# Latent attention: the score scale moved into the query norm's root, row maxima formed negated, and the stage's first twelve products spread over both PSUM bank sets

## The chip, the cores and the metric

The kernel runs on one core of a Trainium2 chip. A core has TensorE (matrix products, written into PSUM), VectorE, ScalarE and GpSimd (element by element work), and DMA queues that bring weights from memory. PSUM has eight banks of 128 x 512 float32 values here. The metric is the device time of one execution in microseconds (us); the median of several runs is compared.

## The reference

The program is a two-layer streaming encoder step: 512 new frames with 16 meta tokens in front (the prompt), and 32 frames of a running stream with 256 past frames (the sample). Each layer is a half-step feed-forward block, a mixer and another half-step feed-forward block. The mixer of the first layer is a gated linear attention; that of the second is a multi-head latent attention (MLA), which the change concerns:

```python
cq, ckv, kr = split(xn @ w_down, ...)            # 384, 256, 64 columns
q = (rmsnorm(cq, q_norm) @ w_uq).reshape(B, L, 8, 128 + 64)
q_nope, q_rope = q[..., :128], apply_rope(q[..., 128:], pos)
ckv = rmsnorm(ckv, kv_norm); kr = apply_rope(kr, pos)
q_lat = einsum('blhn,rhn->blhr', q_nope, w_uk)
s = (q_lat . keys_lat + q_rope . keys_rope) * scale      # scale = 192 ** -0.5
p = softmax(where(mask, s, -inf))
o = einsum('bhqk,bkr->bqhr', p, keys_lat)                # then w_uv and w_out
```

The mask is causal in chunks of 64 frames. The score is linear in the query, and the query is linear in the root 1/sqrt(mean square) of its norm, one number for each frame.

## The kernel before

All activations stand feature by frame: 128 partitions by 560 columns (512 prompt frames, 32 sample frames, 16 meta tokens). Every float32 product is made of three matmuls on operands split into a high and a low part (lines 429, 430 and 432 in `mm`, 436 to 438 in `mm3`); `split` (lines 381, 382) makes the two parts, a ScalarE cast and a VectorE subtraction. Columns are worked in two halves (272 each for queries, `HALF_Q`; 264 each for keys).

PSUM in the mixers is two sets of tiles in one pool: `ps` with three banks, for large products, and `s` with five, for scores, transposes and small things. `self.bank()` asks for one of `ps`, `self.bank("s")` for one of `s`. A tile of a set waits until an earlier tile of the same set has been read.

The MLA goes: latent, rotary key and query projections; `query_roots` and `query_norm` for each half (sum of squares by TensorE, `rsqrt` on VectorE, transposes on TensorE to spread the root over all partitions, a ScalarE copy into `yq` at line 1174, and two GpSimd products at line 1176 that fold the root into the cosine and sine tables). The norm's root is not multiplied into the projections' input but into each query product when it is read from PSUM: `plain` (line 1246) with `yq`, `rotary` through the cosine and sine tables (`rope`, lines 1043 to 1048).

`attention` then runs over eight heads. Its opening is a fixed list: keys of head 0 (two products), the second half's `query_roots`, keys of head 1 (two), `query_norm`, two pieces of the values of heads 0 and 1, and `queries(0)` (for each half a rotary product of both heads and a plain product of each): twelve products through `self.bank()`. Then come the scores of head 0 for its four query tiles, with the other three values pieces and `queries(1)` between. After that, each head's list alternates its transposes with the next head's scores, and `weave` spreads the remaining work (keys, values, queries of later heads, the sample's steps, output projection) between them.

`softmax` takes a tile of scores in PSUM (two tiles for the last query tile, which has 528 keys): the row maximum on VectorE (line 1057), the maximum of two parts (1059), times minus the scale (1060), the exponential on ScalarE with that as bias and the scale as factor, summing as it goes (1062), the sums' addition (1065), reciprocal (1066), and the product with it (1068). It is called 34 times: 32 tiles of the prompt and two of the sample.

The program's lines give priorities; the framework orders the instructions of each engine when the program is built, by what it estimates to be ready. So an engine's order in the trace is not always that of the lines: matmuls of two products can be mixed.

Of the kernel before, what the change touches and what calls it, by code (L numbers as in the profile page):

```python
# [13 lines left out]
AF = mybir.ActivationFunctionType  # L14
ALU = mybir.AluOpType
AX = mybir.AxisListType
# [19 lines left out]
SCALE = (128 + 64) ** -0.5  # L36
# [302 lines left out]
class Net:  # L339
# [18 lines left out]
    def psum(self, ffn):  # L358
# [3 lines left out]
        else:  # L362
# [3 lines left out]
                                                             reuse_waits="tile"))  # L366
        self.bufs = dict(Y=2) if ffn else dict(ps=3, s=5)

    def bank(self, tag="ps"):
        if tag not in self.bufs:  # L370
            tag = "Y"
        return self.ps.tile([P, 512], F32, name=tag, tag=tag, bufs=self.bufs[tag])
# [287 lines left out]
    def down(self, i, l, gi, acts, halves, order, after=None):  # L660
# [4 lines left out]
        def piece(m, hf):  # L665
# [3 lines left out]
            n, c = c1 - c0, slice(c0, c1)  # L669
            Y = self.bank()  # L670
            self.mm(Y[:, :n], L[m], 0, acts, halves[hf])
            nc.vector.scalar_tensor_tensor(self.h[:, m, c], Y[:, :n], 0.5, self.h[:, m, c], op0=ALU.mult, op1=ALU.add)  # L672
            if after is not None:
# [72 lines left out]
    def gla(self, xs, begin, side, op, xpool):  # L746
# [6 lines left out]
        if True:  # L753
# [17 lines left out]
            def wout(g):  # L771
# [10 lines left out]
                for m, hf in order:  # L782
                    if m // 2 not in L:
                        L[m // 2] = self.load(("go", g, m // 2))
                    c0, c1 = HALF_T[hf]
                    Y = self.bank()
                    self.mm(Y[:, :c1 - c0], L[m // 2], 4 * (m % 2), outs[2 * g] + outs[2 * g + 1], (c0, c1))
# [264 lines left out]
    def softmax(self, pool, p, parts):  # L1052

        nc = self.nc
        st = pool.tile([P, 8], F32, name="st", tag="st", bufs=4)
        for i, (s, n, c) in enumerate(parts):
            nc.vector.reduce_max(st[:, i:i + 1], s[:, :n], axis=AX.X)
        if len(parts) == 2:
            nc.vector.tensor_tensor(st[:, 0:1], st[:, 0:1], st[:, 1:2], op=ALU.max)
        nc.vector.tensor_scalar(st[:, 2:3], st[:, 0:1], -SCALE, None, op0=ALU.mult)  # L1060
        for i, (s, n, c) in enumerate(parts):
            nc.scalar.activation(p[:, c:c + n], s[:, :n], AF.Exp, bias=st[:, 2:3], scale=SCALE,
                                 accum_out=st[:, 3 + i:4 + i])
        if len(parts) == 2:
            nc.vector.tensor_tensor(st[:, 3:4], st[:, 3:4], st[:, 4:5], op=ALU.add)
        nc.vector.reciprocal(st[:, 5:6], st[:, 3:4])
        n = sum(q[1] for q in parts)
        nc.vector.tensor_scalar(p[:, :n], p[:, :n], st[:, 5:6], None, op0=ALU.mult)
# [35 lines left out]
    def mla(self, xs, turn, side):  # L1104

        nc, tc, a = self.nc, self.tc, self.a
# [5 lines left out]
        if True:  # L1112
            two = gone("ml2", 2)
            kp = brief("mlk")
            if True:
# [9 lines left out]
                norms = {}  # L1125
# [12 lines left out]
                for hf, (c0, c1) in enumerate(HALF_T):  # L1138
                    n = c1 - c0
                    for m in range(2):  # L1140
                        Y = self.bank(("s", "ps")[hf])
# [7 lines left out]
                for hf, (c0, c1) in enumerate(HALF_T):  # L1149
                    n = c1 - c0  # L1150
                    Y = self.bank()
# [15 lines left out]
                yq = self.np_.tile([P, T], F32, name="yn", tag="yn")  # L1167
# [3 lines left out]

                def query_norm(hf):
                    c = slice(*HALF_Q[hf])
                    nc.scalar.copy(yq[:, c], norms.pop(hf)())
                    for t in (self.cos, self.sin):
                        nc.gpsimd.tensor_tensor(t[:, c], t[:, c], yq[:, c], op=ALU.mult)

                L = [self.load(("wd", 3 + m)) for m in range(2)]
                for hf, (c0, c1) in enumerate(HALF_Q):
                    n = c1 - c0  # L1180
                    for m in range(3):
                        if m == 2 and len(L) == 2:
                            L.append(self.load(("wd", 5)))
                        Y = self.bank()
                        self.mm(Y[:, :n], L[m], 0, xs, (c0, c1))
                        if hf == 1 and m < 2:
                            (query_roots, query_norm)[m](0)
                        nc.vector.tensor_tensor(cq[:, m, c0:c1], Y[:, :n], xs.y[:, c0:c1], op=ALU.mult)
                        w = nv[:, wq + m:wq + m + 1]
                        nc.scalar.activation(cqh[:, m, c0:c1], cq[:, m, c0:c1], AF.Copy, scale=w)  # L1190
                        nc.vector.scalar_tensor_tensor(cql[:, m, c0:c1], cq[:, m, c0:c1], w,
                                                       cqh[:, m, c0:c1].bitcast(F32), op0=ALU.mult, op1=ALU.subtract)
                        self.square(cq[:, m, c0:c1], n, hf, m == 0)
# [4 lines left out]
            brief.close()  # L1198
            cqs = [(cqh[:, m, :], cql[:, m, :]) for m in range(3)]
            self.attention(gone, two, cqs, yq, [partial(f, 1) for f in (query_roots, query_norm)], kph, kpl, rph, rpl, ksh, ksl, rsh, rsl, kth, ktl, turn)  # L1200

    def attention(self, gone, two, cqs, yq, query_norm, kph, kpl, rph, rpl, ksh, ksl, rsh, rsl, kth, ktl, turn):
        nc, tc, a = self.nc, self.tc, self.a
# [11 lines left out]
        for t in ee:  # L1215
            nc.gpsimd.memset(t[64:, :].bitcast(F32), 0.0)
        q = {}

        def queries(pr):
            ha, hb = 2 * pr, 2 * pr + 1  # L1220
            W = {}

            def rotary(c0, c1):
                if "r" not in W:
                    W["r"] = self.load(("qr", pr))
                    W["n"] = self.load(("qn", pr))
                    for h in (ha, hb):
                        q[h] = (self.xtile(), self.xtile(), self.xtile())
                n = c1 - c0
                c = slice(c0, c1)  # L1230
                Y = self.bank()
                self.mm(Y[:, :n], W["r"], 0, cqs, (c0, c1))
                qa, qb = self.temp("y"), self.temp("sq")
                self.rope(qb, self.temp("acc"), qa[:64, :n], Y, n, (c0, c1), True)
                for x, h in ((qa, ha), (qb, hb)):
                    r = q[h][2]
                    nc.scalar.copy(r[:64, c], x[:64, :n])
                    nc.vector.tensor_tensor(r[64:, c], x[:64, :n], r[:64, c].bitcast(F32), op=ALU.subtract)

            def plain(j, h, c0, c1):  # L1240
                n = c1 - c0
                c = slice(c0, c1)
                Y = self.bank()
                self.mm(Y[:, :n], W["n"], 3 * j, cqs, (c0, c1))
                qf = self.temp(("vh", "t")[j])
                nc.vector.tensor_tensor(qf[:, :n], Y[:, :n], yq[:, c], op=ALU.mult)
                self.split(q[h][0][:, c], q[h][1][:, c], qf[:, :n])

            return [f for c in HALF_Q for f in (partial(rotary, *c), partial(plain, 0, ha, *c), partial(plain, 1, hb, *c))]

        oS = {}
# [91 lines left out]
        def keys(h):  # L1343
            def half(c0, c1):
                if c0 == 0:
                    kt[h] = two.tile([P, KP], F32R, name="kh", tag="kh"), two.tile([P, KP], F32R, name="kl", tag="kl")
                    W.append(self.load(("uk", h)))
                kh, kl = kt[h]
                Y = self.bank()
                self.mm(Y[:, :c1 - c0], W[0], 0, [(kph[:, r, :], kpl[:, r, :]) for r in range(2)], (c0, c1))  # L1350
                self.split(kh[:, c0:c1], kl[:, c0:c1], Y[:, :c1 - c0])

            W = []
            return [partial(half, 0, KP // 2), partial(half, KP // 2, KP)]

        def values(pr):
            def piece(i):
                if i == 0:
                    W.append(self.load(("uvp", pr)))
                vh, vl = ve  # L1360
                n = P if i < 4 else 64
                c = slice(i * P, i * P + n)
                Y = self.bank()
                for r in range(2):
                    w = tuple(t[:, 2 * r:2 * r + 2, :].rearrange("p a b -> p (a b)") for t in W[0])
                    self.mm3(Y[:n, :256], (kph[:, r, c], kpl[:, r, c]), w, r == 0, r == 1)
                self.split(vh[:n, i, :], vl[:n, i, :], Y[:n, :256])

            W = []
            return [partial(piece, i) for i in range(5)]  # L1370
# [395 lines left out]
```

## Time and profile before

| what | value |
|---|---|
| median of 3 runs | 2033.72 us (2029.69, 2033.72, 2036.91) |
| profiled execution, its own time | 2032.48 us |
| its span, first to last instruction | 2030.7 us |
| mean granted TensorE clock | 0.996 |
| busy: TensorE, VectorE, ScalarE, GpSimd | 2005.6, 1600.0, 1021.6, 53.5 us |
| DMA, mean over the span | 87 GB/s from and to memory |
| L1057, row maxima | 42 operations, median 0.408 us |
| L1060, times minus the scale | 34 operations, median 0.144 us |
| L1174, copy of the root | 2 operations, median 0.384 us |

Rows of the profile name line, engine and operation, the tile written, the tiles read, shape and count; times are in us, in the groups by line also in ns. "[1.80 <-DVE vl L382]" means that the engine stood idle for 1.80 us before this instruction, and that the VectorE instruction of line 382 that writes `vl` came last. PE is TensorE, PEld its weight loads, DVE VectorE, ACT ScalarE, POOL GpSimd, SP the queue that issues DMAs. A matmul's duration in a row is its latency; in a row of matmuls the next starts before the former ends. PEclk is the clock that TensorE was granted, as a share of full speed.

### The profile page before, as it was taken

The page shows a single profiled execution, that of the slowest core. Times are in us where ns is not written, and L with a number is a line of the kernel's source. Part 1 is how long each engine was busy: PE and PEld are TensorE (multiplying, and loading weights), DVE is VectorE, ACT ScalarE, POOL GpSimd, SP SyncE. Part 2 cuts the span into 40 slices and gives each one's busy share as a digit, 9 for nine tenths or more (in the row PEclk, how much of TensorE's full clock was granted, in tenths as well). Part 3 has the DMA queues.
Part 4 walks back from the last instruction along what each step waited for, and adds up shares of the span by engine and source line. Part 5 has one row for each costly group of instructions (what it writes and reads, how often), then busy time and mean ns, then how long its engine had stood idle before and what let it go on. Part 6 is the DMA issues. An engine that isn't in the chain of part 4 may idle for free.

```text
span 2030.7 us, 38170 instructions
## 1 busy us (share of the span) xinstructions
PE 2005.6 (99%) x15422; PEld 1976.2 (97%) x15422; DVE 1600.0 (79%) x2995; ACT 1021.6 (50%) x1862; POOL 53.5 (3%) x121
## 2 busy tenths in 40 slices
PE   9999999999999999999999999999999999999998
PEld 9999999989999999999999999999989999999998
DVE  8878788566558988788788877886798898888884
ACT  7444445465446544444555444454576575444453
POOL 0000000111110000000000000000110000000000
PEclk9999999999999999999999999999999999999999
DMA  5232322222222132323313333323111413333221
GB/s 184 77 109 85 104 84 81 80 81 71 68 86 92 66 107 90 98 84 105 104 51 106 100 94 95 98 75 98 60 56 44 146 31 100 110 94 98 95 74 66
DMA packets 91969, 180.16 MB, mean 89 GB/s; under 512 B 10176, under 2 KB 22080, under 8 KB 91792
## 3 DMA queue, kind: packets, MB, share of 16 engines
q1 hardware_dynamic: 87328, 172.48, 26.6%
q10 hardware_dynamic: 4464, 5.24, 0.8%
q8 instruction: 121, 1.98, 0.4%
q14 instruction: 56, 0.46, 0.1%
HBM read 173.69 MB, written 3.99 MB: 87 GB/s over the span
## 4 chain that ended last, share of the span: by engine, by line
PE 81%; DVE 12%; DMA 2%; ACT 2%; issue 1%; POOL 0%; SPq 0%; DVEq 0%; ACTq 0%; POOLq 0%
PE Y L432 8%; PE Y L429 8%; PE Y L430 8%; PE A L430 5%; PE A L432 5%; PE A L429 5%; PE ps L429 4%; PE C L432 4%; PE C L430 4%; PE C L429 4%; PE ps L432 4%; PE ps L430 4%; PE B L430 3%; PE B L432 3%; PE B L429 3%; DVE wlo L382 3%
## 5 line engine op out<-in xcount | busy, mean ns | idle before, releaser
L429 PE MATMUL Y<-ah,whi 128*128 128x280 f32 (+1 forms) x1408 | 373.7, 292 | 2.7 <-ACT ah L381 2.2
L430 PE MATMUL Y<-ah,wlo 128*128 128x280 f32 (+1 forms) x1408 | 372.8, 291 | 0.0
L382 DVE TENSOR_TENSOR wlo<-fr,whi 128x1024 fp32r<-128x1024 f32 (+1 forms) x298 | 357.9, 1211 | 15.9 <-ACT whi L381 15.6
L381 ACT CAST whi<-fr 128x1024 fp32r<-128x1024 f32 (+1 forms) x298 | 308.8, 1045 | 103.7 <-PE C L432 40.3
L430 PE MATMUL A<-x,wlo 128*128 128x280 f32 (+1 forms) x1024 | 271.7, 291 | 1.9 <-DVE wlo L382 1.8
L429 PE MATMUL A<-x,whi 128*128 128x280 f32 (+1 forms) x1024 | 272.2, 291 | 1.0 <-ACT x L181 1.0
L429 PEld LDWEIGHTS Y<-ah,whi 128*128 128x128 f32 x1408 | 265.4, 189 | 3.8 <-ACT ah L381 3.2
L672 DVE SCALAR_TENSOR_TENSOR h<-Y,h 128x280 f32<-128x280 f32 (+1 forms) x320 | 141.1, 444 | 159.0 <-PE Y L432 158.5
L430 PEld LDWEIGHTS Y<-ah,wlo 128*128 128x128 f32 x1408 | 266.3, 189 | 0.0
L382 DVE TENSOR_TENSOR wlo<-raw,whi 128x512 fp32r<-128x512 f32 (+5 forms) x231 | 195.0, 846 | 74.8 <-ACT whi L381 69.9
L381 ACT CAST whi<-raw 128x512 fp32r<-128x512 f32 (+5 forms) x231 | 169.6, 736 | 160.1 <-PE ps L432 47.5
L432 PE MATMUL Y<-al,whi 128*128 128x280 f32 (+1 forms) x1408 | 233.0, 291 | 0.0
L300 DVE TENSOR_TENSOR fr<-fr 128x1024 f32<-128x1024 f32 x160 | 195.2, 1220 | 19.5 <-DMA fr<-W 18.1
L432 PEld LDWEIGHTS Y<-al,whi 128*128 128x128 f32 x1408 | 199.4, 188 | 0.0
L430 PEld LDWEIGHTS A<-x,wlo 128*128 128x128 f32 x1024 | 192.7, 188 | 2.8 <-DVE wlo L382 2.8
L429 PEld LDWEIGHTS A<-x,whi 128*128 128x128 f32 x1024 | 192.6, 188 | 1.9 <-ACT x L181 1.2
L430 PE MATMUL B<-x,wlo 128*128 128x280 f32 (+1 forms) x704 | 186.5, 291 | 0.6 <-DVE wlo L382 0.4
L429 PE MATMUL B<-x,whi 128*128 128x280 f32 (+1 forms) x704 | 186.8, 291 | 0.1
L430 PE MATMUL C<-x,wlo 128*128 128x280 f32 (+1 forms) x704 | 186.0, 290 | 0.0
L429 PE MATMUL C<-x,whi 128*128 128x280 f32 (+1 forms) x704 | 186.0, 290 | 0.0
L432 PE MATMUL A<-x,whi 128*128 128x280 f32 (+1 forms) x1024 | 172.9, 290 | 0.6 <-DVE x L182 0.6
L536 ACT COPY r<-A 128x560 f32<-128x560 f32 (+1 forms) x120 | 74.8, 623 | 159.0 <-PE A L432 158.1
(419 smaller groups left out, 4151.7 us busy)
## 6 DMA issues: line engine op xcount, KB each, us to landing
fr<-W SPq DMA_DIRECT2D x351, 256.0 KB, 3.4
raw<-W SPq DMA_DIRECT2D x80, 512.0 KB, 3.5
raw<-W SPq DMA_DIRECT2D x100, 256.0 KB, 2.9
raw<-W SPq DMA_DIRECT2D x40, 128.0 KB, 2.1
raw<-W SPq DMA_DIRECT2D x4, 384.0 KB, 3.0
h<-xT SPq DMA_DIRECT2D x2, 560.0 KB, 6.5
o_y<-h SPq DMA_DIRECT2D x4, 272.0 KB, 2.3
o_y<-h ACTq DMA_DIRECT2D x4, 272.0 KB, 2.5
```

The costliest lines, as they stand in the source:

```text
L300: self.net.nc.vector.tensor_tensor(r[out], r[x], r[y], op=ALU.add)
L381: self.nc.scalar.copy(hi, src)
L382: self.nc.vector.tensor_tensor(lo, src, hi.bitcast(F32), op=ALU.subtract)
L429: f(hi[:, b0 + k, :], xh[:, c], start=not more and k == 0, stop=False)
L430: f(lo[:, b0 + k, :], xh[:, c], start=False, stop=False)
L432: f(hi[:, b0 + k, :], xl[:, c], start=False, stop=k == n - 1)
L536: nc.scalar.copy(r[:, :, :n], of[:, :, :n])
L672: nc.vector.scalar_tensor_tensor(self.h[:, m, c], Y[:, :n], 0.5, self.h[:, m, c], op0=ALU.mult, op1=ALU.add)
```

## The change

The score scale is multiplied into the query norm's root (`query_norm`), and reaches the scores through `yq` and the scaled cosine and sine tables. `softmax` then needs no scale: the row maxima are formed negated, the two parts are joined by a minimum, and the result is the exponential's bias at once. In `attention` a local `bank()` gives the first twelve products that ask for one the sets ps, s, s, ps, s, s, and so on (four times `ps`, eight times `s`), and `ps` to all later ones; the query, key and value products use it.

```diff
@@ softmax
         for i, (s, n, c) in enumerate(parts):
-            nc.vector.reduce_max(st[:, i:i + 1], s[:, :n], axis=AX.X)
+            nc.vector.reduce_max(st[:, i:i + 1], s[:, :n], axis=AX.X, negate=True)
         if len(parts) == 2:
-            nc.vector.tensor_tensor(st[:, 0:1], st[:, 0:1], st[:, 1:2], op=ALU.max)
-        nc.vector.tensor_scalar(st[:, 2:3], st[:, 0:1], -SCALE, None, op0=ALU.mult)
+            nc.vector.tensor_tensor(st[:, 0:1], st[:, 0:1], st[:, 1:2], op=ALU.min)
         for i, (s, n, c) in enumerate(parts):
-            nc.scalar.activation(p[:, c:c + n], s[:, :n], AF.Exp, bias=st[:, 2:3], scale=SCALE,
-                                 accum_out=st[:, 3 + i:4 + i])
+            nc.scalar.activation(p[:, c:c + n], s[:, :n], AF.Exp, bias=st[:, 0:1], accum_out=st[:, 3 + i:4 + i])
@@ query_norm
-                    nc.scalar.copy(yq[:, c], norms.pop(hf)())
+                    nc.scalar.activation(yq[:, c], norms.pop(hf)(), AF.Copy, scale=SCALE)
@@ attention
+        tags = [("ps", "s", "s")[i % 3] for i in range(12)]
+
+        def bank():
+            return self.bank(tags.pop(0) if tags else "ps")
@@ rotary and plain (in queries), half (in keys), piece (in values)
-                Y = self.bank()
+                Y = bank()
```

More of the change, by code (lines that the diff above doesn't have):

```diff
@@ L1242, in plain @@
                 c = slice(c0, c1)
-                Y = self.bank()
+                Y = bank()
                 self.mm(Y[:, :n], W["n"], 3 * j, cqs, (c0, c1))
@@ L1348, in half @@
                 kh, kl = kt[h]
-                Y = self.bank()
+                Y = bank()
                 self.mm(Y[:, :c1 - c0], W[0], 0, [(kph[:, r, :], kpl[:, r, :]) for r in range(2)], (c0, c1))
@@ L1362, in piece @@
                 c = slice(i * P, i * P + n)
-                Y = self.bank()
+                Y = bank()
                 for r in range(2):
```

## The prediction

> **What bounds the kernel now.** I read the page first: engine totals and the chain that ended last.
>
> ```profile
> span 2030.7 us, 38170 instructions
> PE 2005.6 (99%) x15422; PEld 1976.2 (97%) x15422; DVE 1600.0 (79%) x2995; ACT 1021.6 (50%) x1862; POOL 53.5 (3%) x121
> PE 81%; DVE 12%; DMA 2%; ACT 2%; issue 1%; POOL 0%; SPq 0%; DVEq 0%; ACTq 0%; POOLq 0%
> ```
>
> TensorE is the bound over the whole span: only 25.1 us (2030.7 - 2005.6) are without a matmul. A change that leaves the matmuls alone can win only where TensorE stands still or runs slowly. So next I cut the attention stage, which holds every edited line, into stretches; then one cut around the clock's dip.
>
> ```profile
> core 0: us, PE busy (x) PEld busy (x) DVE busy (x) ACT busy (x) POOL busy (x), PEclk, DMA share, GB/s
> 1456.00:1476.00 20.00, 18.07 (x140) 17.02 (x139) 16.68 (x46) 13.98 (x34) 7.69 (x19) 1.00 0.21 58
> 1476.00:1486.00 10.00, 10.00 (x66) 9.98 (x67) 8.65 (x30) 6.75 (x20) 0.78 (x1) 0.83 0.38 113
> 1486.00:1520.00 34.00, 31.20 (x221) 28.37 (x219) 32.21 (x106) 26.34 (x76) 4.76 (x13) 1.00 0.11 32
> 1520.00:1560.00 40.00, 39.82 (x308) 38.90 (x309) 34.22 (x110) 24.60 (x74) 1.45 (x5) 1.00 0.24 72
> 1560.00:1600.00 40.00, 38.01 (x287) 36.48 (x286) 37.88 (x111) 26.76 (x72) 3.10 (x9) 1.00 0.26 78
> sum 164.00, PE 157.10 PEld 149.91 DVE 145.20 ACT 108.05 POOL 17.78; mean PE 26.18 PEld 24.99 DVE 24.20 ACT 18.01 POOL 2.96
> ...
> 1477.00:1480.50 3.50, 3.50 (x16) 3.48 (x15) 2.72 (x11) 2.44 (x8) 0.09 (x1) 0.51 0.52 154
> ```
>
> Over 1456 to 1620 TensorE is without a matmul for 6.9 us (164.0 - 157.1; counted by weight loads 14.1). From 1477.0 to 1480.5 it ran at a granted clock of 0.51, which costs 3.5 x 0.49 = 1.7 us. So 6.9 + 1.7 = 8.6 us, 0.4% of the time, is what this stage can give; by weight loads 15.8. In 1486 to 1520 and 1560 to 1600 VectorE is 95% busy (32.21 of 34, 37.88 of 40): there it sets the pace. Then the waits, to see who is late.
>
> ```profile
> PE ps L429 <- DVE vl L382: 1.8, 1, 1.8
> PE ps L429 <- DVE st L1060: 1.4, 1, 1.4
> PE s L436 <- DVE st L1060: 0.5, 1, 0.5
> ...
> ACT p L1062 <- DVE st L1060: 15.7, 14, 3.4
> ```
>
> Two causes are touched by the change: a product that wants a `ps` bank still unread by the values' subtraction (vl), and the small operation of L1060 in each softmax.
>
> **The banks.** The timeline of TensorE shows where the bank is missed, and one later wait to compare.
>
> ```profile
> 1468.34 0.54 PE L432 MATMUL ps<-cql,whi 128*128 128x272 f32 x3
> 1468.97 0.39 PE L429 MATMUL ps<-cqh,whi 128*128 128x272 f32 x1
> ...
> 1473.81 0.28 PE L438 MATMUL ps<-wlo,kph 128*64 128x256 f32 x1
> 1475.89 0.40 PE L429 MATMUL ps<-cqh,whi 128*128 128x272 f32 x1 [1.80 <-DVE vl L382]
> ...
> 1568.07 0.39 PE L429 MATMUL ps<-x,whi 128*128 128x272 f32 x1 [1.43 <-DVE st L1060]
> ```
>
> With three `ps` banks, the twelve leading products (four of the keys, two of the values, six of queries(0)) reuse a bank after two others. At 1468.97 the twelfth begins at most 0.1 us later than its predecessor's last records end (1468.34 + 0.54): nearly nothing. The 1.80 us at 1475.89 belong to the first product of queries(1), which is not among the twelve. It wants the bank of the third values product. The change helps it only indirectly: eight of the twelve go to `s`, so the three remaining values products find all of `ps` free, can run earlier, and their cast and subtraction can be placed earlier. What stands against it is VectorE:
>
> ```profile
> 1465.65 0.44 DVE L1044 TENSOR_TENSOR acc<-ps,cos 128x272 f32<-128x272 f32 x1 [1.46 <-ACT sq L1043]
> ...
> 1471.28 0.44 DVE L1044 TENSOR_TENSOR acc<-ps,cos 128x272 f32<-128x272 f32 x1 [0.36 <-ACT sq L1043]
> 1472.12 0.43 DVE L1047 TENSOR_TENSOR y<-acc,sq 64x272 f32<-64x272 f32 x1 [0.40 <-POOL sq L1045]
> 1472.48 0.43 DVE L1246 TENSOR_TENSOR t<-ps,yn 128x272 f32<-128x272 f32 x1
> ...
> 1475.41 0.42 DVE L382 TENSOR_TENSOR vl<-ps,vh 128x256 fp32r<-128x256 f32 x1
> ...
> 1480.91 0.44 DVE L1246 TENSOR_TENSOR vh<-ps,yn 128x272 f32<-128x272 f32 x1 [0.99 <-PE ps L432]
> ```
>
> Its 1.46 us before 1465.65 end on ScalarE's rotary copies, which more banks do not hasten. The holes of 0.36 and 0.40 us just about take a 0.42 us subtraction each; the rest of queries(0) fills the time up to 1475.41. Bounds for the banks: a gain of 0 (the subtraction comes no earlier) and one of 1.80 + 1.7 = 3.5 us (wait and slow clock both vanish). As a loss: the three values' subtractions put ahead of the second half of queries(0) delay that by 3 x 0.42 = 1.3 us. I take VectorE's own idle time in 1476 to 1486, 10.00 - 8.65 = 1.35 us: behind that stretch VectorE paces the stage, so a TensorE further ahead would only wait later. 0.99 us of it is VectorE waiting for one of the slow products. So **-1.3 us**, on the condition that the clock's dip goes. The 1.43 us wait before 1568.07 lies in a stretch whose clock is 1.00, so a wait shortened by some 0.4 us should pass without a dip. What is late next: the second-half query subtractions on VectorE, for which scores(0,2) waits.
>
> [...]
>
> **The softmax.** The rows of the maximum, the removed operation and its neighbours:
>
> ```profile
> L1057 DVE TENSOR_REDUCE st<-s x42: 285/408/576, 1475.8 to 1607.5; 128x1 f32<-128x272 f32 x16, 128x1 f32<-128x144 f32 x8, 128x1 f32<-128x400 f32 x8, 128x1 f32<-128x256 f32 x8
> L1060 DVE TENSOR_SCALAR st<-st x34: 132/144/156, 1476.3 to 1608.5; 128x1 f32<-128x1 f32 x34
> ...
> 1475.75 0.30 DVE L1057 TENSOR_REDUCE st<-s 128x1 f32<-128x144 f32 x1
> 1476.30 0.14 DVE L1060 TENSOR_SCALAR st<-st 128x1 f32<-128x1 f32 x1
> 1476.48 0.38 ACT L1062 ACTIVATE p<-s,st 128x144 f32<-128x144 f32 x1 [0.62 <-DVE st L1060]
> ...
> 1498.27 0.15 DVE L1060 TENSOR_SCALAR st<-st 128x1 f32<-128x1 f32 x1
> 1498.34 0.68 DVE L382 TENSOR_TENSOR pTl<-s,pTh 128x512 fp32r<-128x512 f32 x1
> ...
> 1486.00:1520.00 34.00, 1.45 (x10) 1.00 0.11 32
> 1560.00:1600.00 40.00, 1.45 (x10) 1.00 0.26 78
> ```
>
> The change removes 34 operations of 0.144 us. Their successor starts 0.07 us after them (1498.27 to 1498.34), so each occupies VectorE for 0.07 us: 34 x 0.07 = 2.4 us in all. Only in the two stretches where VectorE paces TensorE does that shorten the time; they hold 10 + 10 of the 34: 20 x 0.07 = 1.4 us. Elsewhere the matmuls cover it (39.82 of 40 us busy in 1520 to 1560). Besides, the exponential can start on the maximum itself: the maximum ends at 1476.05 (1475.75 + 0.30), the small operation at 1476.44, the exponential starts 0.04 us later; without the step it starts 0.39 us earlier. ScalarE's 15.7 us of waiting shrink, but ScalarE is not the bound (26.34 of 34); what counts are the two TensorE waits that name L1060, 1.4 and 0.5 us, each 0.39 us shorter: 0.8 us. Together **-2.2 us**. Bounds: 0, if the negated maximum is dearer by what was saved or VectorE stays late for another reason; and 2.4 + 1.4 + 0.5 = 4.3 us, if all three terms count in full. I lean to the middle, as both waits end on a VectorE that has other work queued. The minimum in place of the maximum (L1059) and the exponential without its scale are the same instructions; I cost them at nothing.
>
> [...]
>
> **The root of the query norm.** A copy becomes an activation with a constant scale, twice.
>
> ```profile
> L1190 ACT ACTIVATE cqh<-cq,nv x6: 518/523/524, 1443.4 to 1457.9; 128x272 fp32r<-128x272 f32 x6
> ...
> 1465.59 0.39 ACT L1174 COPY yn<-s 128x272 f32<-128x272 f32 x1
> 1466.01 0.43 DVE L1246 TENSOR_TENSOR vh<-ps,yn 128x272 f32<-128x272 f32 x1
> ```
>
> The nearest activation of that width, with a column as its scale, takes 0.523 us, so at most 0.13 us each, at least nothing. The second reaches VectorE: its product with the root starts 0.03 us after the copy ends. I take **+0.1 us**. No instruction, transfer or queue entry is added; the DMAs stay where they were.
>
> Sum: -1.3 - 2.2 + 0.1 = -3.4 us on the profiled execution's 2032.48 us: **2029.1 us**. The median of the three runs, 2033.72, lies 1.2 us above that execution; against it this is -0.2%. A measurement of this kernel can hardly tell a change under 0.3% (6.1 us) from none.
>
> **The rivals.**
>
> (a) More goes than my sum: the build orders every engine's instructions anew from the first of the twelve products, and with banks to spare and a shorter softmax most of the stage's idle time could close. All 6.9 us and the slow clock's 1.7 give 2032.5 - 8.6 = **2023.9 us**; the bound of 6.1 us is passed when seven tenths of it go. For it: the idle is in few, named places. Against it: in 74 of those 164 us VectorE is 95% busy, and 1.4 to 2.4 us is all that it loses.
>
> [...]
>
> (c) Slower: `s` runs short. Its five banks now hold query products beside the root's tiles and the scores; where the last of the twelve is read late, scores(0,2) or scores(0,3) waits for a bank, TensorE stands and the clock falls. One such stop has been priced above: 1.80 + 1.7 = 3.5 us. Two of them: 2032.5 + 7.0 = **2039.5 us**. It decides once the read of the twelfth product slips past the start of scores(0,2). Against it: that read was at 1472.48, and TensorE did not take up the first product after its stop until 1475.89, over 3 us later.
>
> **How the numbers follow.** My forecast (2 to 6 us faster) has 0.36; (b), within 2 us of before, 0.24; a small loss, one stop of (c), 0.06: together 0.66 within 0.3%. (a) passing 6.1 us has 0.24, (c) with two stops 0.10. The likeliest gives 2029.1. Its own range is 2026.5 to 2031.1. The full one reaches down past (a), for the larger idle counted by weight loads, to 2021.5, and up to 2037.0, one stop of (c) (2036.0) and 1 us of scatter.
>
> **What would show it.** In the new profile: L1060's 34 operations gone, and the maximum still near 0.408 us; ScalarE's 15.7 us of waiting lower and now on L1057. Around 1474 the products of values(0) before the first softmax's scores or right behind, the 1.80 us wait on vl under 1.4 us, and no stretch at 0.51. VectorE still 93% or busier in 1486 to 1520. If the dip is still there, the banks' term is wrong; if the waits merely move from vl to another VectorE operation at equal length, VectorE was the bound earlier than I placed it; if new waits name a read of a query product in `s`, (c) holds. A changed order far behind the attention, in the last feed-forward block, would make the forecast wrong in a way that no row here prices.

## The result and the profile after

The changed kernel takes 2028.68 us (median of 22 runs, 2026.15 to 2031.94) against 2030.70 us of the kernel before (22 runs beside it). The ratio is 0.9988, with a 95% interval of 0.9983 to 0.9994: 2.4 us or 0.12% faster, 1.2 to 3.5 us by the interval (the two medians alone differ by 2.0 us). It is a gain, clear of the scatter and well within 0.3%.

The page of the changed kernel; the lines answer to those shown of before:

```profile
span 2028.0 us, 38139 instructions
PE 2003.5 (99%) x15422; PEld 1974.6 (97%) x15422; DVE 1597.3 (79%) x2961; ACT 1021.4 (50%) x1862; POOL 53.8 (3%) x121
PE 85%; DVE 9%; DMA 2%; ACT 2%; issue 1%; POOL 0%; SPq 0%; DVEq 0%; ACTq 0%; POOLq 0%
```

VectorE has 34 instructions less (2995 to 2961), the other engines the same number. Stretches of the attention stage, changed kernel:

```profile
core 0: us, PE busy (x) PEld busy (x) DVE busy (x) ACT busy (x) POOL busy (x), PEclk, DMA share, GB/s
1456.00:1476.00 20.00, 18.94 (x151) 18.38 (x150) 17.97 (x50) 14.11 (x35) 7.08 (x19) 1.00 0.25 71
1476.00:1486.00 10.00, 9.43 (x73) 8.84 (x71) 8.88 (x28) 8.40 (x24) 2.36 (x4) 1.00 0.23 84
1486.00:1520.00 34.00, 30.94 (x221) 28.57 (x221) 32.50 (x98) 25.84 (x78) 4.34 (x10) 1.00 0.17 51
1560.00:1600.00 40.00, 39.10 (x292) 37.46 (x291) 36.30 (x100) 25.04 (x67) 2.94 (x9) 1.00 0.28 86
```

The stretch at half clock is gone (1.00 where 0.83 stood). VectorE is busy 1.3 us more in the first 20 us (17.97 against 16.68) and in 1486 to 1520 is as full as before. The waits of TensorE in the stage, changed kernel:

```profile
PE s L436 <- ACT p L1061: 2.4, 3, 1.2
PE s L1306 <- DVE psm L1066: 0.9, 1, 0.9
PE ps L429 <- DVE t L1248: 0.9, 1, 0.9
PE s L468 <- DVE ry L509: 0.7, 1, 0.7
```

Neither the 1.8 us on `vl` nor the 1.4 us on `st` is left; scores now wait for a bank of `s` that an exponential still reads.

Spans of single executions also differ outside the stage (it starts at 1453.5 to 1458.2 us in the profiles below). So I measure inside it: from the first weight load of the transposition that ends the projections (L1196 before, L1194 after) to the first matmul group of each head's weighing of values (`weigh`), and to the last addition of the output projection to `h`. Before, then after:

```profile
L1196 PEld LDWEIGHTS s<-ident,cn x2: 94/95/96, 1456.9 to 1457.0; 128*32 128x32 f32 x2
L1416 PEld LDWEIGHTS ps<-pTh,vh x8: 187/188/189, 1498.0 to 1617.9; 128*128 128x128 f32 x8
L1447 DVE TENSOR_TENSOR h<-ps,h x48: 414/431/444, 1539.5 to 1645.4; 128x272 f32<-128x272 f32 x48
```
```profile
L1194 PEld LDWEIGHTS s<-ident,cn x2: 94/95/96, 1456.6 to 1456.7; 128*32 128x32 f32 x2
L1418 PEld LDWEIGHTS ps<-pTh,vh x8: 187/188/189, 1495.9 to 1614.7; 128*128 128x128 f32 x8
L1449 DVE TENSOR_TENSOR h<-ps,h x48: 421/430/444, 1536.8 to 1642.2; 128x272 f32<-128x272 f32 x48
```

The first weighing comes at 41.1 us before (1498.0 - 1456.9) and 39.3 after, the stage's end at 188.5 and 185.6: 1.8 us are won in the opening, 2.9 us in all (differences of rows that show tenths can be off by 0.1 us). The 1.1 us between come in two places: from the first to the second weighing it takes 16.8 us before and 16.4 after, from the fourth to the fifth 25.1 and 24.5. From there on the lead stays level.

Why the opening is shorter: the build put the rotary products of both halves ahead of the values. Changed kernel, first TensorE, then VectorE:

```profile
1460.72 0.28 PE L429 MATMUL ps<-cqh,whi 128*128 128x272 f32 x1
```
```profile
1463.74 0.44 DVE L1044 TENSOR_TENSOR acc<-ps,cos 128x272 f32<-128x272 f32 x1 [0.75 <-ACT sq L1043]
1467.84 0.44 DVE L1044 TENSOR_TENSOR acc<-ps,cos 128x272 f32<-128x272 f32 x1 [0.24 <-POOL cos L1174]
```

Before, that product came behind the first two values pieces:

```profile
1462.67 0.29 PE L429 MATMUL ps<-cqh,whi 128*128 128x272 f32 x1
```

The first rotary product starts 4.1 us into the stage instead of 5.8 (1460.72 - 1456.6; 1462.67 - 1456.9), so its ScalarE copies end earlier, and VectorE's idle time before its first rotary operation falls from 1.46 to 0.75 us. The four values pieces that now follow cover what is left of the rotary chain but for two waits of TensorE, 0.38 and 0.68 us. Two of them, the third and the fourth piece, run first and in `ps`, beginning with the row below. Before, they ran only behind the first scores, and the third one's subtraction was the `vl` that TensorE waited for:

```profile
1462.98 0.28 PE L436 MATMUL ps<-whi,kph 128*128 128x256 f32 x1
```

### The profile page after: what moved, and what is told of

The parts are those of the page before. It is cut to its first block, busy times and chain, and to the rows that moved or that the text cites. A ratio compares the mean times of both kernels' runs of the same rounds, so it can differ in the third digit from the quotient of the medians.

```text
span 2028.0 us, 38139 instructions
## 1 busy us (share of the span) xinstructions
PE 2003.5 (99%) x15422; PEld 1974.6 (97%) x15422; DVE 1597.3 (79%) x2961; ACT 1021.4 (50%) x1862; POOL 53.8 (3%) x121
## 4 chain that ended last, share of the span: by engine, by line
PE 85%; DVE 9%; DMA 2%; ACT 2%; issue 1%; POOL 0%; SPq 0%; DVEq 0%; ACTq 0%; POOLq 0%
PE Y L432 8%; PE Y L429 8%; PE Y L430 8%; PE A L430 6%; PE A L432 5%; PE A L429 5%; PE C L432 4%; PE C L430 4%; PE C L429 4%; PE ps L429 4%; PE B L430 4%; PE ps L432 4%; PE ps L430 4%; PE B L432 4%; PE B L429 4%; DVE wlo L382 3%
## 5 line engine op out<-in xcount | busy, mean ns | idle before, releaser
L381 ACT CAST whi<-fr 128x1024 fp32r<-128x1024 f32 (+1 forms) x298 | 308.8, 1045 | 104.0 <-PE C L432 39.1
L430 PE MATMUL B<-x,wlo 128*128 128x280 f32 (+1 forms) x704 | 186.5, 291 | 0.6 <-DVE wlo L382 0.6
```

The source lines that it names most:

```text
L381: self.nc.scalar.copy(hi, src)
L430: f(lo[:, b0 + k, :], xh[:, c], start=False, stop=False)
```

## The experiments

The stage offsets come from the profiled execution of each kernel, the times from its runs beside the kernel before. "VectorE" is its busy time in the first 18 us of the stage, "half clock" the time within the stage for which TensorE was granted half its clock in that one execution.

| kernel | time, ratio to before (interval) | VectorE, first 18 us | first weighing | end of stage | half clock |
|---|---|---|---|---|---|
| before | 1 | 14.7 | 41.1 | 188.5 | 3.4 |
| the change | 0.9988 (0.9983 to 0.9994) | 16.0 | 39.3 | 185.6 | 0 |
| softmax_only | 0.9998 (0.9989 to 1.0007) | 14.8 | 41.0 | 187.7 | 3.4 |
| banks_only | 0.9990 (0.9981 to 0.9999) | 16.0 | 39.1 | 186.5 | 0 |
| filler | 0.9993 (0.9984 to 1.0002) | 14.7 | 40.9 | 188.1 | 0 |
| rotary_first | 1.0011 (1.0002 to 1.0020) | 15.9 | 40.7 | 190.3 | 0 |
| rotary_early | 1.0014 (1.0006 to 1.0023) | 14.4 | 42.1 | 191.6 | 3.4 |
| opening_ps | 1.0033 (1.0021 to 1.0045) | 14.0 | 43.7 | 193.3 | 6.8 |
| plain_in_s | 1.0001 (0.9992 to 1.0010) | 14.5 | 41.1 | 188.5 | 3.4 |
| extra_small | 1.0033 (1.0021 to 1.0046) | 14.7 | 43.4 | 195.3 | 3.4 |
| keys_values_in_s | 0.9987 (0.9979 to 0.9996) | 15.8 | 39.1 | 186.4 | 0 |
| small_op_in_head_5 | 1.0002 (0.9993 to 1.0011) | 14.7 | 40.3 | 187.7 | 0 |
| banks_21 | 0.9999 (0.9990 to 1.0008) | 15.4 | 40.6 | 189.5 | 6.8 |
| keys_values_softmax | 0.9993 (0.9984 to 1.0002) | 15.8 | 39.0 | 185.7 | 0 |

**The two halves of the change, each alone.** My theory: the gain is the opening's, by the banks. The rival: it is the 34 operations that VectorE no longer does.

> The scale in the norm's root and the negated maxima alone; all twelve products in ps as before. If the gain comes from the opening order that the banks allow, this one keeps the 1.80 us wait of the first product of queries(1) and the stretch at about half clock, and gains 0 to 1 us. If it comes from the 34 removed VectorE operations, it gains 1.4 to 2.4 us, nearly all that the whole change gave.

> The bank sets alone; softmax and root as before. If the opening order makes the gain, both rotary products of queries(0) stand before the values, no wait over 1.4 us and no stretch at half clock is left between 1470 and 1482, and the time falls by 1.5 to 3 us. If the removed operations make it, the time falls by at most 0.5 us.

softmax_only is the new `softmax` and `query_norm` with `self.bank()` everywhere; banks_only is the list of sets with the softmax of before. The banks win 2.0 us of the stage, all of it before the first weighing; the softmax 0.8 us, nearly none of it there. 2.0 + 0.8 is the whole change's 2.9 within 0.1, so at the stage's end the two add up. The timed ratios say the same, more coarsely. The waits of softmax_only:

```profile
PE ps L429 <- DVE vl L382: 1.8, 1, 1.8
PE s L436 <- ACT p L1061: 1.5, 2, 0.9
PE ps L429 <- DVE t L1243: 0.9, 1, 0.9
```

The wait on `vl` stands as before. The theory held.

**Is it the clock?** The dip at 0.51 cost TensorE 1.7 us. An execution in which the wait before it is filled, and the dip does not come, shows what the dip alone is worth.

```diff
+        def filler():
+            d = self.bank("s")
+            for i in range(14):
+                pe.matmul(d[:, :256], kph[:, 0, :P], kph[:, 1, :256], start=i == 0, stop=i == 13)
+
-        weave([partial(scores, 0, t) for t in range(4)], v0[2:] + queries(1))
+        weave([partial(scores, 0, t) for t in range(4)], v0[2:] + [filler] + queries(1))
```

> The kernel before with 14 extra matmuls of 256 columns (some 1.7 us) into an s bank that nobody reads, in the place of the 1.80 us wait. They shorten no wait of the real work. If the wait itself drops the clock, the stretch at 0.51 goes and the time falls by 1 to 1.7 us although there is more work. If the clock's dip has another cause, it stays, and the time is the same or up to 0.3 us longer.

The opening of filler in three stretches from the stage's start, 8, 10 and 22 us long, columns as in the table of stretches above:

```profile
1454.40:1462.40 8.00, 8.00 (x65) 7.60 (x64) 6.64 (x23) 5.40 (x15) 1.27 (x8) 1.00 0.38 118
1462.40:1472.40 10.00, 9.89 (x78) 9.49 (x77) 8.10 (x18) 7.58 (x20) 4.88 (x9) 1.00 0.02 6
1472.40:1494.40 22.00, 19.72 (x148) 18.52 (x147) 20.88 (x68) 17.85 (x48) 4.71 (x11) 1.00 0.17 57
```

The clock stays at 1.00, and the last scores of head 0 come 1.5 us earlier (24.4 us into the stage instead of 25.9). But the first weighing comes only 0.2 us earlier and the end 0.4: VectorE, busy for the same 14.7 us in the first 18, takes the gain back. The timed interval holds both no gain and the expected 1 us. So in this stage the dip's 1.7 us of TensorE time are worth 0.2 us at the first weighing and 0.4 at the end, against 2.0 at either place for the banks alone: most of the banks' gain is not the clock. That the wait brings the dip is not shown by this one execution: small_op_in_head_5, below, waits 1.80 us at the same place and has no dip either.

**Is it the order, without the banks?** Three kernels move work by hand, with all products in `ps`.

> The kernel before with one edit: in the fixed opening list the two rotary products of queries(0) come before the root's spreading and the values; all products stay in ps. If the early rotary products are what the banks bring, the wait of 1.80 us shortens, the stretch at half clock goes, and the time falls by 1.5 to 3 us without a bank of s. If the free banks themselves are needed, the values stall on ps instead, and the time stays within 0.5 us of before.

```diff
-        for f in keys(0) + query_norm[:1] + keys(1) + query_norm[1:] + v0[:2] + queries(0):
+        q0 = queries(0)
+        for f in keys(0) + query_norm[:1] + keys(1) + q0[:1] + q0[3:4] + query_norm[1:] + v0[:2] + q0[1:3] + q0[4:]:
```

In rotary_first the second half's rotary queries of heads 0 and 1 are formed from tables that do not hold the norm's root yet: that factor is left out there. The other two keep it:

> The kernel before with the opening list in another order and no bank of s: after the root's spreading, both rotary products of queries(0), then the two values pieces, then the plain products. The order keeps the computation. If starting the rotary work earlier is the whole of what the banks bring, the first weighing of head 0 comes 1.5 to 2 us earlier and so does the end of the stage. If the banks themselves are needed, products stall on ps, and the gain at the first weighing is under 0.7 us.

```diff
+        for f in keys(0) + query_norm[:1] + keys(1) + query_norm[1:] + q0[:1] + q0[3:4] + v0[:2] + q0[1:3] + q0[4:]:
```

> The order that the changed kernel got, written by hand with ps alone: rotary products, four values pieces, plain products; the second row of scores right after the first. If the order is all, it gains like the banks alone, about 2 us. If three banks are too few for it, waits of some 0.4 to 1.3 us on reads of ps tiles stand between 1462 and 1472 and eat most of that.

```diff
+        for f in keys(0) + query_norm[:1] + keys(1) + query_norm[1:] + q0[:1] + q0[3:4] + v0[:4] + q0[1:3] + q0[4:]:
...
+        rest = [[], v0[4:] + q1[:1], q1[1:3], q1[3:]]
+        for t in range(4):
+            scores(0, t)
+            for f in rest[t]:
+                f()
```

All three are slower. TensorE in rotary_early now waits inside the opening for a rotary product to be read out of `ps`:

```profile
1468.93 0.39 PE L429 MATMUL ps<-cqh,whi 128*128 128x272 f32 x1 [1.72 <-DVE acc L1044]
1470.84 0.45 PE L429 MATMUL ps<-cqh,whi 128*128 128x272 f32 x1 [0.52 <-DVE vl L382]
```

A rotary product holds its bank for the ScalarE copies and a VectorE operation; two of them leave one `ps` bank of three. VectorE starves (14.4 and 14.0 us), and the first weighing slips by 1.0 and 2.6 us; opening_ps also runs 3.4 us longer at half clock than before, which may be part of that. rotary_first escapes most of the slip (first weighing 0.4 us early). All three lose another 1.8 to 1.9 us between the first and the second weighing (18.6 to 18.8 us in place of 16.8), where the build chose another order; which edit of the order does that stays open. My expectation that the order alone is enough fell, and so did the other one for rotary_first, a time within 0.5 us of before.

**Are free banks enough without the order?**

> Banks of s for the four plain query products alone; keys, values and rotary products stay in ps. The matmul order of the opening stays that of before but for the spreading of the root, while ps is free for the values. If free banks without a new order are enough, the wait on vl falls under 1 us and the first weighing comes 1.5 to 2 us earlier. If the new order is what gains, the gain at the first weighing is under 0.7 us and the time the same within 1 us.

```diff
+        tags = ["ps"] * 6 + ["ps", "s", "s"] * 2
```

No. The values still come first, `vl` still makes TensorE wait, nothing changes:

```profile
PE ps L429 <- DVE vl L382: 2.0, 1, 2.0
```

**And which banks are needed?**

> Softmax as before; of the twelve products only two key products and the two values pieces take banks of s, all six query products stay in ps. The rotary products again come ahead of the values. If the early rotary work is enough once the keys hold no ps bank, VectorE is busy for 9.4 of 10 us from 8 to 18 us after the stage's start as with the whole bank change, and the stage ends 2 us earlier. If the plain products need s as well, they stall on ps behind the rotary products, VectorE stays near 8 us, and the stage gains under 0.7 us or loses.

```diff
+        tags = ["ps", "s", "s", "ps", "s", "s"] + ["ps"] * 6
```

These four products in `s` give the whole effect of the banks: first weighing 39.1, end 186.4, ratio 0.9987. The first rotary product again starts 4.1 us into the stage (at 1457.9):

```profile
1462.03 0.28 PE L429 MATMUL ps<-cqh,whi 128*128 128x272 f32 x1
```

My reading, which no run takes apart further: with half of the keys out of `ps`, the rotary products get `ps` banks as soon as they can run, ahead of the values; all six query products then do with `ps`. So early rotary work and somewhere else for the values are needed together.

**More banks still.**

> The changed kernel with the pattern of bank sets carried on to 21 products, so through the other three values pieces and queries(1). If more spare banks let TensorE run further ahead, the lead at the first weighing grows from 1.8 to 2.5 us or more and the time falls by up to 1 us against the changed kernel. If VectorE is full by then, or s runs short for the scores, nothing is won, or 1 to 3 us are lost.

Longer is worse: the lead at the first weighing shrinks from 1.8 to 0.5 us and the stage ends 1.0 us after that of the kernel before. Its waits:

```profile
PE s L436 <- ACT p L1061: 2.3, 2, 1.5
PE s L436 <- DVE vh L1248: 1.7, 1, 1.7
PE s L1306 <- DVE psm L1066: 1.7, 1, 1.7
```

The line with `vh` L1248 is the prediction's rival (c) seen: scores wait for a bank of `s` in which a query product stands unread. That is the smaller part of the loss. Another 2.3 us go between the second and the third weighing (19.7 us in place of 17.4), where the line with `psm` lies. Each of these two waits (1.72 us before 1482.63, 1.71 us before 1517.20) is followed by some 3.4 us at half clock, from about 1484.3 and 1518.4 on (steps of 0.21 to 0.23 us between matmuls that before and behind take 0.11 to 0.13); how the loss divides between waits and clock was not tried.

**Where the softmax gains.** Of its 0.8 us, 0.6 fall between the fourth and fifth weighing, beside the 1.43 us wait before 1568.07.

> The scale in the root and the negated maxima, all products in ps, and one small VectorE operation put back in the four softmaxes of head 5 alone, whose third stands next to the wait of 1.43 us near 1568. If the softmax change gains only at that wait, the stage's gain of 0.8 us falls to 0.3 us or less. If it gains by VectorE time everywhere, it stays at 0.7 us.

```diff
+        if again:
+            nc.vector.tensor_scalar(st[:, 0:1], st[:, 0:1], 1.0, None, op0=ALU.mult)
...
-            self.softmax(at, pt[t], parts)
+            self.softmax(at, pt[t], parts, h == 5)
```

Four operations put back bring the wait back, and the step between these weighings is 25.1 us again, not 24.4 as in softmax_only:

```profile
1565.19 0.40 PE L429 MATMUL ps<-x,whi 128*128 128x272 f32 x1 [1.42 <-DVE st L1061]
```

The end of the stage does not show it by itself, because this execution had no clock dip in the opening and was already 0.7 us ahead of softmax_only at the first weighing (40.3 against 41.0). From there to the end it takes 147.4 us, as before, and 146.7 in softmax_only. So of the 34 removed operations those of this head paid, and the others next to nothing. How they pay is open: the operation put back beside the wait runs behind the read that ends it, so its own time is not what delays the product; VectorE's order ahead of the wait also differs between the two kernels. softmax_only still waits 0.87 us there, on `t`, the query product's read:

```profile
1563.95 0.39 PE L429 MATMUL ps<-x,whi 128*128 128x272 f32 x1 [0.87 <-DVE t L1243]
```

**The other direction.**

> The kernel before with three more small multiplications by one behind L1060 in each softmax, 102 in all, in the chain to the exponential. If such an operation costs VectorE's occupied 0.07 us wherever VectorE paces the stage, 60 of them add 4 us. If what counts is only the wait that ends on L1060 near 1568, the time grows by the chain there, 3 x 0.14 to 3 x 0.4 us, so 0.4 to 1.2 us. If an operation costs its whole 0.144 us, 8 us or more.

```diff
         nc.vector.tensor_scalar(st[:, 2:3], st[:, 0:1], -SCALE, None, op0=ALU.mult)
+        for _ in range(3):
+            nc.vector.tensor_scalar(st[:, 2:3], st[:, 2:3], 1.0, None, op0=ALU.mult)
```

The stage grows by 6.8 us (195.3 - 188.5), the ratio says 6.7 (4.3 to 9.3): 0.067 us for each of the 102, between the expected 4 and 8 us. Removing 34 gave 0.024 us each. The growth is not even, as a price for each operation would make it: 2.3 us are there at the first weighing, 2.7 more come between the second and the third, 0.6 in the next step, 1.2 between the sixth and the seventh and little elsewhere. The step with the wait of 1.43 us stays at 25.1 us, so the expectation that only this wait counts fell too. Adding and removing are not mirror images here: I take it that three dependent operations lengthen chains to an exponential, while the removed one mostly lay under other waits. How the 6.8 us divide between VectorE's time and those chains was not tried.

**Both together, smaller.**

> The changed softmax and root with s for two key products and the two values pieces alone. If the bank term (2.1 us at the stage's end by keys_values_in_s) and the softmax term (0.6 us between the weighings of heads 3 and 4) are independent, the stage ends 2.7 us earlier than before, as in the changed kernel, and the time is that of the changed kernel within 1 us, 0.12 to 0.14% below before. If the new order breaks the softmax term, the stage gains 2.1 us or less.

The stage ends at 185.7: the terms are independent (2.1 + 0.7 = 2.8). Its time, 2028.83 us, is not told apart from the changed kernel's; its ratio of 0.9993 is short of the expected 0.12%, with an interval that holds that and no gain. No version here beats the changed kernel by a measurable amount.

## Why the prediction was right, point by point

*The total.* Forecast 2029.1 us, 3.4 us under the profiled execution; measured 2.4 us (1.2 to 3.5) by the ratio and 2.9 by the stage. The direction and "within 0.3%" held, and the size lies within the forecast of 2 to 6 us. The terms did not each hold: the banks gave 0.7 us more than forecast, the softmax 1.4 us less, and these errors of opposite sign half cancelled. It is luck besides that the median, 2028.68 us, comes within 0.4 us of 2029.1: the forecast counted from 2032.48 us, 1.8 us above the median of before, 2030.70. And a change under 0.3% could be told: the interval of 22 runs is about 0.06% to either side.

*The banks: -1.3 us forecast, -2.0 measured.* The right idea was that VectorE's idle time limits the gain. The step that failed is "its 1.46 us before 1465.65 end on ScalarE's rotary copies, which more banks do not hasten". They did: the build brought the rotary product, and with it the copies, 1.7 us forward. The forecast took the order ahead of the wait that names a bank as given. Its other idea came true, that the later values products find `ps` free and run earlier: the wait on `vl` is gone. The idle time to be won was put in 1476 to 1486; there VectorE is busy only 0.2 us more (8.88 against 8.65), and 1.3 us more before 1476.

*The condition on the clock.* The dip went, as required. filler shows that it was worth 0.2 us at the first weighing and 0.4 at the end. softmax_only, with a dip, against small_op_in_head_5, without one, which have the same matmul order up to there, show 0.7 at the first weighing and 0.6 at the third (75.1 and 74.5 us). So of the banks' 2.0 us at the stage's end 0.4 to 0.6 can be the dip's, and about 1.5 are left for the order. Here are their waits at the same place and the stretch behind each, first softmax_only, then small_op_in_head_5 (granted clock in the third column from the right):

```profile
1472.52 0.39 PE L429 MATMUL ps<-cqh,whi 128*128 128x272 f32 x1 [1.81 <-DVE vl L382]
```
```profile
1472.50:1476.50 4.00, 3.98 (x17) 3.96 (x18) 3.04 (x12) 2.81 (x9) 0.00 (x0) 0.57 0.33 80
```
```profile
1473.84 0.39 PE L429 MATMUL ps<-cqh,whi 128*128 128x272 f32 x1 [1.80 <-DVE vl L382]
```
```profile
1472.80:1494.80 22.00, 19.18 (x144) 18.28 (x145) 20.82 (x64) 18.10 (x49) 4.80 (x12) 1.00 0.20 57
```

*The softmax: -2.2 us forecast, -0.8 measured.* The failed term is 20 x 0.07 = 1.4 us for the stretches in which VectorE is 95% busy: the lead of softmax_only over before is 0.2 us or less at the first four weighings and 0.8 to 0.9 from the fifth on. A busy engine did not mean that each operation taken from it shortened the stage. The other term, 0.8 us for two waits that name L1060, was about right in size (0.6 to 0.7 at one of them), but not in its way, an exponential that starts earlier. The name misled: the product at 1568.07 waited for a bank that `t` had to be read from (1567.58 to 1568.01), and L1060 (from 1567.93) was only VectorE's operation right behind it.

*The root: +0.1 forecast.* The activation takes 0.393 us where the copy took 0.384: nothing. The negated maximum takes 0.418 us in the median (0.408 before), 0.4 us more over 42 of them against the 2.4 us of VectorE time saved: so a maximum dearer by what was saved, the softmax's lower bound, is out.

*The rivals.* (a) did not come: most of the idle time was not to be had. (b), a time within 2 us of before, came true for the softmax alone: most of its 2.2 us stayed hidden, 0.8 came. The whole change's 2.4 us (1.2 to 3.5) lies around that limit. (c) did not come in the changed kernel, but in banks_21, with its 1.7 us wait and the half clock behind it.

## What to carry to other kernels

A wait on a bank tells where the shortage ends, not what a bank would bring: ask which work the order puts earlier once the bank is there, and whether it feeds the engine that is the bound. Here a long chain (copies, table product, two sums) started 1.7 us earlier and filled VectorE; the order without the banks lost, the banks without the order won nothing, and with more banks the scores waited. Time taken from a 95% busy engine counted only where another engine was seen waiting for it.

## What the runs showed of the hardware

A TensorE wait of 1.8 us was followed by some 3.4 us at half clock in some executions and not in others: 1.80 us with a dip to 0.51 (before) and 1.81 us with 0.57 over 4 us (softmax_only), 1.80 us without any (small_op_in_head_5, 1.00 from 1472.8 to 1494.8), and 1.79 us without any at the same place in extra_small (1.00 from 1456 to 1486). Shorter waits stood ahead of a dip too: in softmax_only, behind the stage, the clock fell to 0.51 behind two waits of 0.37 and 0.74 us, while no dip followed the single wait of 1.43 us before 1568.07 in the kernel before (1.00 from 1560 to 1600):

```profile
1676.58 0.39 PE L429 MATMUL Y<-ah,whi 128*128 128x272 f32 x1 [0.37 <-DVE h L672]
1677.71 0.50 PE L430 MATMUL A<-x,wlo 128*128 128x272 f32 x1 [0.74 <-DVE wlo L382]
1677.80:1681.30 3.50, 3.50 (x16) 3.50 (x17) 2.36 (x5) 0.42 (x1) 0.00 (x0) 0.51 0.63 191
```

So in these executions the length of the last wait does not decide alone; what else does is not shown.

What such a stretch costs can be read in the attention stage alone: half speed for 3.4 us, 1.7 us of lost TensorE time, left 0.2 us (filler against before) to 0.7 us (softmax_only against small_op_in_head_5) at the first weighing, the next point where VectorE's work was needed. Ahead of the stage, before and the changed kernel have one such stretch each, near 989 us (0.53 over 988.8 to 992.3, 0.54 over 988.9 to 992.4), behind a wait of 1.91 and 1.92 us for `ah`, and begin the stage at 1456.9 and 1456.6 us; the other profiles begin it at 1453.5 to 1458.2 us, and how much of that spread goes to such stretches is not shown. Over whole executions the time goes with the mean granted clock: of the 33 of before beside softmax_only, eight with 0.998 have a median of 2030.0 us, five with 0.995 one of 2034.0; over all 33 time and clock have a correlation of -0.88.
